# Output projections by Strassen's algorithm over pairs of token blocks, and stage buffers in pools that take turns

## The chip, the cores and the metric

The kernel runs on one core of a Trainium2 chip. Its engines are TensorE (PE; its weight loads are listed as PEld), VectorE (DVE), ScalarE (ACT) and GpSimd (POOL); SyncE (SP) issues nearly all transfers. Each engine works through its own queue in order and waits on semaphores. The metric is the device time of one execution in microseconds, as the median of several runs; a profiled execution gives the trace, whose span runs from the first to the last instruction.

## The reference

Two layers of gated attention over 2048 prompt tokens and 64 sample tokens, width 1024, 16 heads of 64. Layer 0 (here A) attends to a window of its own and two earlier chunks with two key/value heads and learned sinks; layer 1 (B) to its own and eight earlier chunks with 16 heads. In each layer the attention's output, times a gate, goes through a square output projection and is added to the layer's input:

```python
y_p = x_p + (op * jax.nn.silu(gp)) @ w_out      # (2048 x 1024) @ (1024 x 1024)
...
y_s = x_s + (os_ * jax.nn.silu(gs)) @ w_out     # (64 x 1024) @ (1024 x 1024)
```

Everything is float32. The outputs are the tokens after both layers and the newest keys and values.

## The kernel before, in words

All activations lie transposed (features on partitions, tokens along the free dimension). A product of two float32 matrices is made of three matmuls in a faster type: each operand is split into a high part (a cast on ScalarE) and a low part (the operand less its high part, on VectorE for weights, on GpSimd for activations), and high x high, high x low and low x high are added up in PSUM. So 128 rows of outputs, 128 features of input and one block of tokens cost three matmuls.

The order of TensorE's instructions is written out by hand. Attention is a pipeline over its items, and a `Filler` (L615) hands out matmuls of independent jobs between attention's steps, so that TensorE has work while VectorE and ScalarE do the softmax. Its jobs stand in one list: layer A's input projections, layer A's output projections, layer B's input projections, layer B's output projections. `Filler.to(mark)` runs jobs up to a mark; marks are sums of ideal matmul times. The other engines' queues are ordered by the framework's scheduler, which places an instruction by its own estimate of times.

The 2112 tokens are cut into 8 blocks of 264 (`OT`). An output job (`output_jobs`, L1251) is one block and one half of the 1024 output features: it loads the gated attention output of its block in four pieces of 256 features (`load_act`, L351; the piece `xraw` is cast at L385 and its low part made at L386), and for each of four groups of 128 output features runs 8 x 3 = 24 matmuls of 264 columns into one PSUM bank `pj` (L1283 to L1285), adds the layer's input `res` on VectorE (L1288) and stores pairs of groups (L1290). Weights of a half come in eight pieces of 512 columns, cast at L307, low part at L308. There are 16 such jobs in a layer, first the 8 blocks of half 0, then those of half 1. In each layer the last attention items are interleaved with the first output jobs, and the rest of the jobs runs alone. Layer B's input jobs need all of layer A's blocks that they read.

SBUF tiles of all stages come from one pool `sb`; keys, values and their low parts (`KA`, `KB`, `VT` and others) are constants that stay for the whole kernel. PSUM has the pools `pp` and, for attention, `pa` or `pb`.

## Time and profile before

| | |
|---|---|
| median of 3 runs | 2325.57 us (2324.6 to 2330.49) |
| profiled execution, span | 2323.8 us |
| matmuls | 13981, of which 3072 in output projections |
| TensorE busy | 2269.6 us |
| VectorE, ScalarE, GpSimd busy | 1547.3, 1432.7, 847.6 us |
| output projections from, to (layer A) | 659.4 to 863.2 us |
| output projections from, to (layer B) | 2110.7 to 2320.0 us |

The profiled execution's own time is its span; the median of the runs is 1.8 us above it. Matmuls are pipelined, so a matmul's duration is longer than the distance to the next one: what a matmul costs is read from the distance of starts. An engine's busy time includes time in which an instruction has started and cannot get on.

### The profile page before, as it was taken

The numbers are of one execution on the slowest core, as the hardware profiler recorded it, in microseconds if no ns is written. First come the engines' busy times: TensorE is split into PE (matmuls) and PEld (weight loads), VectorE is DVE, ScalarE is ACT, GpSimd is POOL, SyncE is SP. The second block draws the span as 40 slices with busy tenths as digits, with TensorE's granted clock in tenths as the row PEclk, the third lists the DMA queues.
The fourth block names the chain that finished last, engine by engine and source line by source line (L and its number), as shares of the span: only waits on it lengthen the run. The fifth ranks groups of instructions, "written<-read, shape, count | busy, mean of one in ns | idle before, by whom it ended". The sixth has DMA issues, their size and how long they took to land.

```text
span 2323.8 us, 42433 instructions
## 1 busy us (share of the span) xinstructions
PE 2269.6 (98%) x13981; PEld 1985.2 (85%) x13981; DVE 1547.3 (67%) x5214; ACT 1432.7 (62%) x3644; POOL 847.6 (36%) x1194
## 2 busy tenths in 40 slices
PE   8899999999999998999999999999999999999999
PEld 7787888888889997878888888888888888888999
DVE  7679988887782228876766767767667677676211
ACT  7778777777772236765665656656656566566321
POOL 5554533333254446432222222222222222224443
PEclk9999999999999999999999999999999999999999
DMA  8846446754446776453444533534435435433664
GB/s 256 263 146 207 162 144 195 229 167 162 134 126 204 226 216 219 145 186 126 158 142 128 161 127 114 178 126 152 143 123 163 134 103 177 131 126 106 189 186 148
DMA packets 232126, 379.37 MB, mean 163 GB/s; under 512 B 24721, under 2 KB 163361, under 8 KB 231873
## 3 DMA queue, kind: packets, MB, share of 16 engines
q1 hardware_dynamic: 231904, 376.65, 51.3%
q8 instruction: 110, 1.80, 0.3%
q14 instruction: 112, 0.91, 0.1%
HBM read 296.13 MB, written 82.08 MB: 163 GB/s over the span
## 4 chain that ended last, share of the span: by engine, by line
PE 77%; DVE 10%; ACT 5%; DMA 5%; issue 2%; POOL 1%; SPq 0%; POOLq 0%; ACTq 0%; DVEq 0%
PE pj L481 13%; PE pj L483 12%; PE pj L482 12%; PE pj L1283 5%; PE pj L1284 5%; PE pj L1285 5%; PE sb L597 5%; PE o L1189 3%; PE o L1188 3%; PE tp L597 3%; PE sb L1110 3%; PE sb L1111 3%; PE sa L597 2%; DVE sq L524 1%; DVE p L1114 1%
## 5 line engine op out<-in xcount | busy, mean ns | idle before, releaser
L481 PE MATMUL pj<-wh,xx 128*128 128x512 f32 (+1 forms) x1648 | 668.7, 406 | 15.2 <-DVE ms L433 7.2
L483 PE MATMUL pj<-wh,xx 128*128 128x512 f32 (+1 forms) x1648 | 638.1, 387 | 0.0
L482 PE MATMUL pj<-wl,xx 128*128 128x512 f32 (+1 forms) x1648 | 635.0, 385 | 0.0
L483 PEld LDWEIGHTS pj<-wh,xx 128*128 128x128 f32 x1648 | 310.4, 188 | 67.3
L481 PEld LDWEIGHTS pj<-wh,xx 128*128 128x128 f32 x1648 | 311.9, 189 | 56.9 <-ACT pb L504 6.5
L386 POOL TENSOR_TENSOR xx<-xraw,xx 128x528 fp32r<-128x528 f32 (+1 forms) x200 | 265.6, 1344 | 218.2 <-ACT xx L385 212.0
L482 PEld LDWEIGHTS pj<-wl,xx 128*128 128x128 f32 x1648 | 312.5, 190 | 37.7
L528 POOL TENSOR_TENSOR f<-f,mhalf 128x4 f32<-128x4 f32 (+3 forms) x221 | 227.9, 1031 | 228.7 <-DVE f L524 216.9
L1118 ACT ACTIVATE p<-p,nm 128x640 f32<-128x640 f32 (+5 forms) x272 | 204.4, 751 | 167.2 <-DVE nm L1114 165.1
L1283 PE MATMUL pj<-xx,wh 128*128 128x264 f32 x1024 | 293.3, 286 | 0.1
L1284 PE MATMUL pj<-xx,wh 128*128 128x264 f32 x1024 | 291.3, 284 | 0.0
L1285 PE MATMUL pj<-xx,wl 128*128 128x264 f32 x1024 | 289.8, 283 | 0.0
L1114 DVE CUSTOM_DVE_ANT_0 p<-sb,BT 128x640 f32<-128x640 f32 (+5 forms) x272 | 196.7, 723 | 119.6 <-PE sb L1111 116.2
L570 DVE TENSOR_TENSOR pl<-sb,ph 128x640 fp32r<-128x640 f32 (+5 forms) x288 | 196.8, 683 | 116.1 <-ACT ph L569 113.7
L385 ACT CAST xx<-xraw 128x528 fp32r<-128x528 f32 (+1 forms) x200 | 123.4, 626 | 220.3 <-PE pj L1285 131.9
L984 POOL TENSOR_TENSOR o<-gt,o 128x256 f32<-128x256 f32 (+2 forms) x140 | 107.4, 767 | 371.3 <-issue 149.0
L569 ACT CAST ph<-sb 128x640 fp32r<-128x640 f32 (+5 forms) x288 | 167.1, 580 | 122.4 <-PE sb L597 114.0
L1288 DVE TENSOR_TENSOR res<-pj,res 128x264 f32<-128x264 f32 x128 | 55.1, 431 | 246.5 <-PE pj L1285 230.7
L1283 PEld LDWEIGHTS pj<-xx,wh 128*128 128x128 f32 x1024 | 192.7, 188 | 0.8 <-DVE res L1288 0.3
L1285 PEld LDWEIGHTS pj<-xx,wl 128*128 128x128 f32 x1024 | 192.6, 188 | 0.0
L1284 PEld LDWEIGHTS pj<-xx,wh 128*128 128x128 f32 x1024 | 192.4, 188 | 0.2
L524 DVE CUSTOM_DVE_ANT_0 sq<-pa 128x64 f32<-128x64 f32 (+1 forms) x850 | 170.2, 253 | 22.1 <-ACT pa L504 20.0
(189 smaller groups left out, 4810.5 us busy)
## 6 DMA issues: line engine op xcount, KB each, us to landing
xx<-xsb SPq DMA_DIRECT2D x224, 512.0 KB, 4.1
xx<-xsa SPq DMA_DIRECT2D x88, 512.0 KB, 4.8
xraw<-oga SPq DMA_DIRECT2D x64, 264.0 KB, 3.4
xraw<-ogb SPq DMA_DIRECT2D x64, 264.0 KB, 3.3
xsa<-xx SPq DMA_DIRECT2D x32, 512.0 KB, 4.0
wraw<-in_w_in_b_dram SPq DMA_DIRECT2D x64, 256.0 KB, 3.4
xsb<-xx SPq DMA_DIRECT2D x32, 512.0 KB, 3.8
xraw<-in_x_dram SPq DMA_DIRECT2D x40, 256.0 KB, 4.1
```

The source lines that it names most:

```text
L386: nc.gpsimd.tensor_tensor(xl, rv, xh.bitcast(F32), op=ALU.subtract)
L481: nc.tensor.matmul(ps[:n, :C], xh, wh, start=k == 0, stop=False)
L482: nc.tensor.matmul(ps[:n, :C], xh, wl, start=False, stop=False)
L483: nc.tensor.matmul(ps[:n, :C], xl, wh, start=False, stop=k == KC - 1)
L528: nc.gpsimd.tensor_tensor(fv, fv, mhalf[:n, :H], op=ALU.pow)
L570: b = nc.vector.tensor_tensor(dst_lo, src, dst_hi.bitcast(F32), op=ALU.subtract)
L597: nc.tensor.transpose(out, in_, ident[:n, :n])
L1114: mi = nc.vector.tensor_tensor_reduce(out=p[:n, :nk], in0=S[:n, o : o + nk], in1=bias[:n, b0 : b0 + nk], op0=ALU.add, op1=ALU.min, scale=1 ...
L1118: ex = nc.scalar.activation(p[:n, :nk], p[:n, :nk], AF.Exp, scale=-1.0, bias=nmh, accum_out=it.sm[:n, 2 * i + h : 2 * i + h + 1],)
L1283: nc.tensor.matmul(ps[:, :OT], wh, oh, start=k == 0, stop=False)
L1284: nc.tensor.matmul(ps[:, :OT], wh, ol, start=False, stop=False)
L1285: nc.tensor.matmul(ps[:, :OT], wl, oh, start=False, stop=k == KC - 1)
```

## The change

Half 0 of the first four token blocks is still made directly (`FIRST = 4`). All other output blocks are made by Strassen's algorithm in the form with seven products and fifteen additions. A job is a pair of token blocks and one half of the output features: the operands are 2 x 2 blocks, (two token blocks) x (two halves of the input features) and (two halves of the input features) x (two groups of 256 output features). There are six such jobs in a layer, two in half 0 and four in half 1. A product is 24 matmuls of 264 columns into a PSUM tile `pw` of two banks.

- `weights(half, k)`: the operand of product k on the weights' side. Raw quarters `wq` are loaded once a half; sums and differences of them are made on VectorE, then each operand is split (cast on ScalarE, low part on VectorE).
- `operand(g)`: the same for activations. Raw quarters `oq` are loaded, sums `os` made on VectorE, and the split's low part goes to VectorE for the first of the operand's two pieces and to GpSimd for the second (`LOW_DVE`). Operands are made two products ahead (`AHEAD`).
- `add_job`: after the first product ScalarE copies it to `op1` and GpSimd adds it to three residual tiles `ores`; every later product, or sum of products in the same banks, is added to a residual tile by VectorE. Products 0 to 2 and so on share banks: with the letters "abababa", product 2 is accumulated on product 0's banks, 3 on 1's, 5 on 3's, 6 on 4's, so that a product waits until the addition of the one before it in its banks is done.
- `begin()` starts the stage: raw loads, all seven weight operands and two activation operands are issued while the rest of the direct jobs runs on TensorE.

Attention's tiles and those of the new stages come from pools that are opened and closed stage by stage (`PHASED`): attention A, output A, attention B, output B. A tile of a later stage waits for the tiles of the earlier one that lay in the same place. Constants of attention (`KA`, `VT`, ...) become tiles of their stage, and the queries' zero rows are written once a layer.

```diff
+FIRST = 4
+AHEAD = 2
+LOW_DVE = (0, 2, 4, 6, 8, 10, 12)
+PHASED = {
+    "p", "ph", "pl", "q1", "G", "gt", "o1", "pa", "pb", "sq", "f", "nm", "sm", "ko",
+    "oq", "os", "ores", "op1", "wq", "vh", "vl",
+}
...
-        return sb.tile(shape, dt, tag=tag, name=f"{tag}_{uid[0]}", bufs=bufs)
+        pool = phase[0] if tag in PHASED else sb
+        return pool.tile(shape, dt, tag=tag, name=f"{tag}_{uid[0]}", bufs=bufs)
...
 
-        for j in range(NO):
+        for j in range(FIRST):
             add_unit(j)
+
+    def wino_output(layer, xin, xout):
+        st = Item()
+        st.raw, st.res, st.A, st.q, st.w, st.parts = {}, {}, {}, {}, {}, {}
+        st.open = False
+        todo = [(0, p) for p in range(FIRST // 2, NO // 2)] + [(1, p) for p in range(NO // 2)]
+        w_o = (w_o_a, w_o_b)[layer]
+        T2 = 2 * OT
...
+        def split(src, hi, lo, dve):
+            nc.scalar.copy(hi, src)
+            e = nc.vector if dve else nc.gpsimd
+            e.tensor_tensor(lo, src, hi.bitcast(F32), op=ALU.subtract)
+
+        def weights_raw(half):
+            q = {}
+            for n, k in ((0, 0), (0, 1), (1, 0), (1, 1)):
+                q[n, k] = halves_of("wq", [P, 512], 12)
+                for c, r in enumerate(q[n, k]):
+                    src = w_o[half, 2 * k + c, :, :, 256 * n : 256 * n + 256]
+                    load(r.rearrange("p (k c) -> p k c", k=2), src)
+            st.q[half] = q
+
+        def weights(half, k):
+            q = st.q[half]
+            if k == 1:
+                q["d"] = halves_of("wq", [P, 512], 12)
+                q["s"] = halves_of("wq", [P, 512], 12)
+                for c in range(2):
+                    nc.vector.tensor_tensor(q["d"][c], q[1, 0][c], q[0, 0][c], op=ALU.subtract)
+                    nc.vector.tensor_tensor(q[1, 0][c], q[1, 1][c], q[1, 0][c], op=ALU.subtract)
+                    nc.vector.tensor_tensor(q["s"][c], q[1, 0][c], q[0, 0][c], op=ALU.add)
+            if k == 5:
+                for c in range(2):
+                    nc.vector.tensor_tensor(q["s"][c], q[0, 1][c], q["s"][c], op=ALU.subtract)
+            src = q[((0, 0), "s", (0, 1), (1, 0), "d", "s", (1, 1))[k]]
+            out = []
+            for c in range(2):
+                if k < 3:
+                    wh, wl = (t(n, [P, 2, 256], WN, F32R) for n in ("wh", "wl"))
+                else:
+                    wh, wl = (t(n, [P, 2, 256], 8, F32R) for n in ("vh", "vl"))
+                split(src[c], wh.rearrange("p k c -> p (k c)"), wl.rearrange("p k c -> p (k c)"), True)
+                out.append((wh, wl))
+            st.w[half, k] = out
...
+        def operand(g):
+            i, k = divmod(g, 7)
+            if i >= len(todo):
+                return
+            A = lambda tb, kb: st.A[i, tb, kb]
+            for c in range(2):
+                if k == 1:
+                    if c == 0:
+                        st.A[i, "s1"] = halves_of("os", [P, T2], 4)
+                        st.A[i, "s2"] = halves_of("os", [P, T2], 4)
+                    s1, s2 = st.A[i, "s1"][c], st.A[i, "s2"][c]
+                    nc.vector.tensor_tensor(s1, A(1, 0)[c], A(1, 1)[c], op=ALU.add)
+                    nc.vector.tensor_tensor(s2, s1, A(0, 0)[c], op=ALU.subtract)
+                elif k == 3:
+                    a = A(1, 0)[c]
+                    nc.vector.tensor_tensor(a, A(0, 0)[c], a, op=ALU.subtract)
+                elif k == 6:
+                    s2 = st.A[i, "s2"][c]
+                    nc.vector.tensor_tensor(s2, A(0, 1)[c], s2, op=ALU.subtract)
+            key = ((i, 0, 0), (i, "s2"), (i, 0, 1), (i, 1, 0), (i, "s1"), (i, 1, 1), (i, "s2"))[k]
+            out = []
+            for c, a in enumerate(st.A[key]):
+                xx = t("xx", [P, 4 * OT], XN, F32R)
+                split(a, xx[:, :T2], xx[:, T2:], 2 * k + c in LOW_DVE)
+                out.append((pair(xx[:, :T2]), pair(xx[:, T2:])))
+            st.parts[g] = out
+
+        def begin():
+            st.open = True
+            half = todo[0][0]
+            weights_raw(half)
+            raw(0, (0, 0), (1, 0), (1, 1), (0, 1))
+            residual(0)
+            for k in range(7):
+                weights(half, k)
+                if k < AHEAD:
+                    operand(k)
+                filler.to(min(filler.direct, filler.done + 2.2))
+            filler.to(filler.direct)
+
+        def add_job(i):
+            half, p = todo[i]
+            last = i + 1 < len(todo) and todo[i + 1][0] != half
+
+            def gen():
+                bank = {}
+                view = lambda x: x.rearrange("p (n c) -> p n c", n=2)[:, :, :OT]
+
+                def add(x, r):
+                    nc.vector.tensor_tensor(pair(r), view(bank[x]), pair(r), op=ALU.add)
+
+                def done(tb, nb):
+                    c, o = 4 * half + 2 * nb, (2 * p + tb) * OT
+                    store(xout[:, c : c + 2, o : o + OT], pair(st.res[i, tb, nb]))
+
+                for k in range(7):
+                    g = 7 * i + k
+                    x = "abababa"[k]
+                    if k in (0, 1, 4):
+                        bank[x] = psum("pw", 1024, 2, scores_pool[0])
+                    if k == 2:
+                        raw(i + 1, (0, 0), (1, 0))
+                    elif k == 3:
+                        raw(i + 1, (1, 1))
+                        residual(i + 1)
+                    elif k == 4:
+                        raw(i + 1, (0, 1))
+                    if last and k == 0:
+                        weights_raw(1)
+                    if last and k > 0:
+                        weights(1, k - 1)
+                    if i and k == 0 and todo[i - 1][0] != half:
+                        weights(1, 6)
+                    operand(g + AHEAD)
+                    parts = st.parts.pop(g)
+                    w = st.w[half, k]
+                    first, final = k in (0, 1, 4), k in (2, 5, 6)
+                    for n in range(2):
+                        dst = bank[x][:, 512 * n : 512 * n + OT]
+                        for c in range(4):
+                            oh, ol = (a[:, c % 2, :] for a in parts[c // 2])
+                            wh, wl = (a[:, c % 2, n * P : (n + 1) * P] for a in w[c // 2])
+                            nc.tensor.matmul(dst, wh, oh, start=first and c == 0, stop=False, skip_group_check=True)
+                            nc.tensor.matmul(dst, wh, ol, start=False, stop=False, skip_group_check=True)
+                            nc.tensor.matmul(dst, wl, oh, start=False, stop=c == 3, skip_group_check=True)
+                            if n < 1 or c < 3:
+                                yield 3 * OT / 2400
+                    r = lambda tb, nb: st.res[i, tb, nb]
+                    if k == 0:
+                        p1 = t("op1", [P, T2], 2)
+                        nc.scalar.copy(pair(p1), view(bank[x]))
+                        for tb, nb in ((0, 1), (1, 1), (1, 0)):
+                            nc.gpsimd.tensor_tensor(r(tb, nb), r(tb, nb), p1, op=ALU.add)
+                    elif k == 1:
+                        add(x, r(0, 1))
+                    elif k == 2:
+                        add(x, r(0, 0))
+                        done(0, 0)
+                    elif k == 3:
+                        add(x, r(1, 1))
+                    elif k == 4:
+                        add(x, r(1, 1))
+                        done(1, 1)
+                    elif k == 5:
+                        add(x, r(1, 0))
+                        done(1, 0)
+                    else:
+                        add(x, r(0, 1))
+                        done(0, 1)
+                        for j in (2 * p, 2 * p + 1):
+                            key = ("x1", "y")[layer], j
+                            finished[key] = finished.get(key, 0) + 1
+                    yield 3 * OT / 2400
...
     with tc.manual_schedule(engines={mybir.EngineType.PE}):
         attend_a = layer_a()
-        for half in range(2):
-            output_jobs(0, half, x0, x1)
+        output_jobs(0, 0, x0, x1)
+        direct_a = filler.total
+        output_a = wino_output(0, x0, x1)
         attend_b = layer_b()
-        for half in range(2):
-            output_jobs(1, half, x1, y)
-        with tc.tile_pool(name="pa", bufs=4, space=bass.MemoryType.PSUM) as scores_pool[0]:
-            attend_a()
-        with tc.tile_pool(name="pb", bufs=2, space=bass.MemoryType.PSUM) as scores_pool[0]:
-            attend_b()
-        filler.attending = False
-        filler.to(filler.total)
+        output_jobs(1, 0, x1, y)
+        direct_b = filler.total
+        output_b = wino_output(1, x1, y)
+        for name, work, direct in (
+            ("a", attend_a, None), ("wa", output_a, direct_a), ("b", attend_b, None), ("wb", output_b, direct_b)
+        ):
+            filler.direct = direct
+            filler.attending = False
+            with tc.tile_pool(name="s" + name, bufs=1, reuse_waits="tile") as phase[0]:
+                bufs = 4 if name == "a" else 2
+                with tc.tile_pool(name="p" + name, bufs=bufs, space=bass.MemoryType.PSUM, reuse_waits="tile") as scores_pool[0]:
+                    work()
```

On the engines, the rows show what stands one behind another in a queue. A row is the line, the operation, what it writes and reads, and the size of a row of the output. VectorE before, in the middle of layer A's output jobs (`res` residuals, `pj` a job's PSUM bank, `wl` the low part of weights):

```order
L1288 TENSOR_TENSOR res_10223<-pj_10277,res_10223 128x264
L1288 TENSOR_TENSOR res_10304<-pj_10306,res_10304 128x264
L308 TENSOR_TENSOR wl_10256<-wraw_9987,wh_10255 128x512
L308 TENSOR_TENSOR wl_10263<-wraw_9997,wh_10262 128x512
L308 TENSOR_TENSOR wl_10270<-wraw_10007,wh_10269 128x512
L1288 TENSOR_TENSOR res_10304<-pj_10332,res_10304 128x264
```

Between the weights there are only additions out of PSUM. VectorE now, where layer A's new stage begins (L1307 is the direct jobs' addition, the old L1288; L1338 a low part; L1355 to L1357 sums of weights; L1405 sums of operands; `wl`, `vl` low parts of weights, `xx` of operands):

```order
L1307 TENSOR_TENSOR res_9760<-pj_9762,res_9760 128x264
L1355 TENSOR_TENSOR wq_9697<-wq_9628,wq_9620 128x512
L1356 TENSOR_TENSOR wq_9628<-wq_9632,wq_9628 128x512
L1307 TENSOR_TENSOR res_9760<-pj_9796,res_9760 128x264
L1357 TENSOR_TENSOR wq_9699<-wq_9628,wq_9620 128x512
L1355 TENSOR_TENSOR wq_9698<-wq_9629,wq_9621 128x512
L1338 TENSOR_TENSOR vl_9785<-wq_9628,vh_9784 128x512
L1338 TENSOR_TENSOR xx_9668<-oq_9636,xx_9668 128x528
L1356 TENSOR_TENSOR wq_9629<-wq_9633,wq_9629 128x512
L1338 TENSOR_TENSOR wl_9708<-wq_9699,wh_9707 128x512
L1357 TENSOR_TENSOR wq_9700<-wq_9629,wq_9621 128x512
L1405 TENSOR_TENSOR os_9715<-oq_9640,oq_9644 128x528
```

Sums and low parts of weights stand around the last direct additions; the low part of the first operand, `xx`, comes after eight of the weights' rows. VectorE now, in the middle of the new stage of layer B (L1443 is the addition of a product out of PSUM; L1405 to L1412 are sums of operands):

```order
L1405 TENSOR_TENSOR os_29175<-oq_29025,oq_29061 128x528
L1443 TENSOR_TENSOR ores_28803<-pw_28987,ores_28803 128x528
L1409 TENSOR_TENSOR oq_29025<-oq_29021,oq_29025 128x528
L1338 TENSOR_TENSOR xx_29073<-oq_28797,xx_29073 128x528
L1443 TENSOR_TENSOR ores_28801<-pw_28951,ores_28801 128x528
L1338 TENSOR_TENSOR xx_29111<-os_28913,xx_29111 128x528
L1406 TENSOR_TENSOR os_29177<-os_29175,oq_29021 128x528
L1405 TENSOR_TENSOR os_29176<-oq_29026,oq_29062 128x528
L1409 TENSOR_TENSOR oq_29026<-oq_29022,oq_29026 128x528
L1443 TENSOR_TENSOR ores_28807<-pw_28987,ores_28807 128x528
L1338 TENSOR_TENSOR xx_29143<-oq_29021,xx_29143 128x528
L1406 TENSOR_TENSOR os_29178<-os_29176,oq_29022 128x528
```

The additions out of PSUM now stand between sums and low parts of the next products' operands, those of the next job among them. GpSimd now, where the new stage of layer A begins (L397 is the direct jobs' low part, the old L386; L1338 the low part of the second piece of an operand; L1486 the addition of the first product, `op`, to a residual tile):

```order
L397 TENSOR_TENSOR xx_9500<-xraw_9492,xx_9500 128x528
L1338 TENSOR_TENSOR xx_9671<-oq_9637,xx_9671 128x528
L1486 TENSOR_TENSOR ores_9654<-ores_9654,op_2144_9935 128x528
L1486 TENSOR_TENSOR ores_9656<-ores_9656,op_2144_9935 128x528
L1486 TENSOR_TENSOR ores_9658<-ores_9658,op_2144_9935 128x528
L1338 TENSOR_TENSOR xx_9726<-os_9718,xx_9726 128x528
L1338 TENSOR_TENSOR xx_9908<-oq_9649,xx_9908 128x528
L1338 TENSOR_TENSOR xx_9946<-oq_9641,xx_9946 128x528
```

The three additions of the first product stand ahead of the second product's low part (`xx<-os`).

More of the change, by code (lines that the diff above doesn't have):

```diff
@@ L599, in hybrid_encoder_kernel @@
     halves = [slice(0, 64), slice(64, 128)]
-    Q2 = [const([P, 512], f"q2_{i}", F32R) for i in range(2)]
     turn = [0]
@@ L605, in zero @@
         nc.gpsimd.memset(x.bitcast(F32), 0.0)
-    for q in Q2:
-        zero(q[64:128])
     def low_queries():
         turn[0] += 1
-        return Q2[turn[0] % 2]
+        return own.Q2[turn[0] % 2]
     class Filler:
@@ L700, in take_kv @@
                 kn, v = pr[:n, 0:128], pr[:n, 128:256]
-                split_v(n, v, VS[:, 1] if last else VT[:, tt])
+                split_v(n, v, own.VS[:, 1] if last else own.VT[:, tt])
                 it.knorm = head_norm(n, kn)
@@ L941, in pipeline @@
         def pipeline():
+            attention_tiles("a")
+            for q in own.Q2:
+                zero(q[64:128])
             N = len(items)
@@ L1023, in gen @@
                     v, kn = pr[:n, 256:384], pr[:n, 128:256]
-                    split_v(n, v, VS[:, 2] if last else VT[:, tt])
+                    split_v(n, v, own.VS[:, 2] if last else own.VT[:, tt])
                     it.todo += head_norm(n, pr[:n, 0:256]) + gate(n, it.gate[:n, e])
@@ L1055, in queries @@
             if u == NU:
[L1056 removed]
+                kd = [a[:, CB : CB + TS] for a in (own.KSA, own.KSB)]
             else:
[L1058 removed]
+                kd = [a[:, u * UT : (u + 1) * UT] for a in (own.KA, own.KB)]
             qt = [tp[r, 0:T] for r in halves]
@@ L1201, in pipeline @@
             bg.lazy = True
-            for q in Q2:
+            attention_tiles("b")
+            for q in own.Q2:
+                zero(q[64:128, 0:256])
                 zero(q[0:64, 256:512])
```

99 lines of the change are left out of this document (70 added, 29 removed).

## The prediction

> **What bounds the kernel now.** I read the page's busy times and its chain first, then the two output stages in stretches of time, then each kind of instruction that the change multiplies, and last the stretches in which VectorE and GpSimd work at once.
>
> ```profile
> PE 2269.6 (98%) x13981; PEld 1985.2 (85%) x13981; DVE 1547.3 (67%) x5214; ACT 1432.7 (62%) x3644; POOL 847.6 (36%) x1194
> ...
> PE 77%; DVE 10%; ACT 5%; DMA 5%; issue 2%; POOL 1%; SPq 0%; POOLq 0%; ACTq 0%; DVEq 0%
> ```
>
> TensorE is busy 98% and holds 77% of the chain, so a matmul less is time less, as long as nothing else takes over. The change touches only the output projections. Two stretches inside them (columns: length, then busy us and count by engine, granted clock, DMA share, GB/s):
>
> ```profile
> 720.00:840.00 120.00, 120.00 (x989) 120.00 (x988) 24.42 (x49) 31.78 (x51) 54.07 (x41) 1.00 0.68 203
> 2210.00:2310.00 100.00, 100.00 (x825) 100.00 (x824) 17.38 (x37) 22.30 (x36) 43.71 (x33) 1.00 0.62 178
> ```
>
> TensorE never waits there: 120/989 = 0.121 us a matmul of 264 columns. VectorE is 20% busy, GpSimd 45%. What VectorE does there waits for TensorE, hardly the reverse:
>
> ```profile
> L1288 DVE TENSOR_TENSOR res<-pj,res x128: 400/433/436, 669.6 to 2320.3; 128x264 f32<-128x264 f32 x128
> ...
>   PE pj L1285: 230.7, 100
> ...
>   PEld pj L1283: 0.3, 1
> ```
>
> Where the stages begin and end: the last attention matmul of a layer, and the last output matmul (durations min/median/max, then first and last start, first for layer A, then for layer B).
>
> ```profile
> L931 PE MATMUL o<-pl,VT x22: 389/397/505, 607.5 to 705.6; 128*128 128x512 f32 x22
> L1285 PE MATMUL pj<-xx,wl x512: 278/282/292, 659.7 to 863.2; 128*128 128x264 f32 x171
> ```
>
> ```profile
> L1189 PE MATMUL o<-pl,VT x36: 273/280/334, 2106.2 to 2166.1; 128*128 128x256 f32 x24, 128*128 128x128 f32 x12
> L1285 PE MATMUL pj<-xx,wl x512: 278/282/290, 2111.0 to 2320.0; 128*128 128x264 f32 x171
> ```
>
> So the stretch after attention is 863.2 - 705.6 = 157.6 us in layer A and 2320.0 - 2166.1 = 153.9 us in layer B. The instructions stand in the same order as before on every compute engine outside these stretches, so I leave the rest of the span as it is.
>
> **What is removed.** A layer's projections take 2 x 8 x 96 = 1536 matmuls; now 4 x 96 direct and 6 x 168 in products, 1392. That is 144 x 0.121 = 17.4 us a layer, 34.8 us in all, if TensorE stays the bound.
>
> **What is added, per layer.** VectorE gets 28 low parts of weights, 16 sums of weights, 42 low parts of operands and 48 sums of operands: 134 instructions that read two SBUF tiles, where before there were 8 (the second half's weights, L308). It gets 36 additions out of PSUM of 528 columns for 48 of 264. GpSimd has 42 low parts and 18 additions of the first product, 60 for 48. ScalarE has 15 casts or copies of 528 in a job of seven products. Prices:
>
> ```profile
> L308 DVE TENSOR_TENSOR wl<-wraw,wh x32: 674/693/1825, 512.9 to 2226.5; 128x512 fp32r<-128x512 f32 x32
> L386 POOL TENSOR_TENSOR xx<-xraw,xx x200: 1262/1327/1816, 5.1 to 2307.2; 128x528 fp32r<-128x528 f32 x64, 128x512 fp32r<-128x512 f32 x36
> L385 ACT CAST xx<-xraw x200: 602/633/642, 4.4 to 2306.5; 128x528 fp32r<-128x528 f32 x64, 128x512 fp32r<-128x512 f32 x36
> L570 DVE TENSOR_TENSOR pl<-sa,ph x132: 403/680/693, 60.4 to 702.4; 128x512 fp32r<-128x512 f32 x124, 128x256 fp32r<-128x256 f32 x4, 64x256 fp32r<-64x256 f32 x4
> ```
>
> ScalarE: 15 x 0.63 = 9.5 us in a job whose matmuls take 168 x 0.121 = 20.3 us; never the bound. Transfers: activations and residuals as many as before (64 and 32 a layer), weights 24 for 16; at a landing of 3.4 us they were hidden and stay so once the stage runs.
>
> ```profile
> xraw<-oga SPq DMA_DIRECT2D x64, 264.0 KB, 3.4
> ```
>
> VectorE's first line has a strange spread: median 0.69 us, longest 1.83. The timeline of both engines shows why (start, duration).
>
> ```profile
> 757.11 3.91 POOL L386 TENSOR_TENSOR xx<-xraw,xx 128x528 fp32r<-128x528 f32 x3 [5.14 <-ACT xx L385]
> ```
>
> ```profile
> 769.28 4.40 POOL L386 TENSOR_TENSOR xx<-xraw,xx 128x528 fp32r<-128x528 f32 x3 [5.64 <-ACT xx L385]
> ```
>
> ```profile
> 768.18 1.29 DVE L308 TENSOR_TENSOR wl<-wraw,wh 128x512 fp32r<-128x512 f32 x2 [0.46 <-ACT wh L307]
> 769.76 1.45 DVE L308 TENSOR_TENSOR wl<-wraw,wh 128x512 fp32r<-128x512 f32 x1 [0.28 <-ACT wh L307]
> 771.13 0.42 DVE L1288 TENSOR_TENSOR res<-pj,res 128x264 f32<-128x264 f32 x1
> ```
>
> Three GpSimd instructions alone take 3.91 us, 1.30 each. At 769.76 a VectorE instruction with two SBUF tiles starts behind the first of the three: it takes 1.45 instead of 0.69, and the three take 4.40. They do not overlap; each stands until the other is done. At 771.13 VectorE's addition out of PSUM runs under GpSimd's third instruction at its usual 0.42. So a **pair**, one such VectorE and one GpSimd instruction with both queues full, costs 1.30 + (4.40 - 3.91) = 1.79 us of VectorE's queue. Alone, VectorE's instruction costs 0.61 (two in 1.29, the second ending 0.6 after the first), the addition out of PSUM of 528 columns about 0.62 (0.68 for 512, less the same overlap).
>
> [...]
>
> **The sum.** Per layer VectorE has 60 pairs, 107.4 us; the other 70, once the first four are done, 42.7 us; 36 additions out of PSUM, 22.3 us: 172.4 us in one queue. It cannot start at once: its fifth weight instruction stands behind a direct addition that waits for TensorE, 93 matmuls after attention in layer A (11.3 us), 66 in layer B (8.0 us). In layer A 16 instructions for layer B's first unit and its weights and 4 GpSimd low parts fall in as well: 16 x 0.61 + 4 x 1.18 = 14.5 us. So the stretch lasts 11.3 + 172.4 + 14.5 = 198.2 us in layer A, 8.0 + 172.4 = 180.4 us in layer B. TensorE alone would need 17 + 122 = 139 us. Against 157.6 and 153.9 that is **+40.6 and +26.5, together +67.1 us**: the 34.8 us are lost, and as much twice over. On the profiled execution, 2323.8 + 67.1 = 2390.9; its median run is 2325.57, 1.8 above its span, hence **2392.7, say 2393 us**.
>
> Bounds. Above: all pairs collide as summed and TensorE's own waits add to it. At each start GpSimd's three additions of the first product stand ahead of the low part that the second product needs: product one ends, copy 0.6, three times 1.30, then 1.30: product two starts about 5 us late even with no collision. Where TensorE idles long its clock falls:
>
> ```profile
> 1003.00:1010.00 7.00, 3.47 (x20) 2.75 (x18) 6.62 (x20) 2.09 (x5) 1.77 (x4) 0.90 0.93 316
> 1010.00:1017.00 7.00, 7.00 (x30) 6.33 (x31) 2.86 (x13) 4.03 (x9) 3.22 (x5) 0.61 0.23 73
> ```
>
> After 3.5 us idle the granted clock is 0.61 over the next 7 us, some 2.7 us lost. Five such waits a layer would be 27 us; I take none, because VectorE and not TensorE sets the pace while these waits occur, and keep 20 us for the range. Below: no pair collides. Then VectorE needs 130 x 0.61 + 22.3 = 102 us, TensorE decides, and only the late second product (5 us) and the job in which the second half's weights are made (37 x 0.61 + 6 x 0.62 = 26.3 us for 20.3) are lost: 17.4 - 11 = 6.4 us gained a layer, 13 in all. I take the upper end, because both queues are long and in order, and nothing makes GpSimd wait for VectorE's gaps.
>
> The pools that take turns: the first weights land where old keys lay, the first operands where the last values lay, so those loads wait for attention's last matmul. 17 us of direct matmuls cover them (3.4 us each landing, 16 in a row): zero, up to 5 us a layer where the queue is slow. At the end a single 528 column addition stands for one of 264, +0.2 us.
>
> **Rivals.**
> - *Half hidden.* GpSimd's instructions run under the 36 PSUM additions and while VectorE waits for casts. For it: at 771.13 they do overlap. Against: GpSimd too waits for casts, and the adds stand between others. It takes at most 22.3 us a layer off: 2393 - 45 = 2348 us.
> - *TensorE stays the bound* (the other side). Collisions are rare since the engines drift apart. Decisive count in layer A: 11.3 + 102 + 14.5 + 1.18 c = 157.6 gives c = 25 of 60; under some 25 to 40 collisions a layer is no longer than before. At none: 2325.6 - 13 = 2313 us; with the start's waits hidden too, 2291. For it: GpSimd is idle a third of a job (10 x 1.30 = 13 us of 20.3). Against: VectorE is then at 15 x 0.61 + 6 x 0.62 = 12.9 us of the same 20.3, the two sums with the pairs' loss do not fit in 20.3, and the weights' job is over it already.
> - *The waits add up.* Loads at the start and the falling clock come on top: 2393 + 20 = 2413, at worst 2430 us.
>
> **How the numbers follow.** Forecast (2370 to 2412) 0.58, half hidden 0.20, the waits add up 0.12, TensorE stays the bound 0.10. About 0.3%, 7 us, is what a measurement of this kernel tells from no change. Faster takes 0.07 of the last case; within 0.3% takes its remaining 0.03 and 0.02 of the half hidden one; slower has 0.88. The range, 2345 to 2425, leaves out the last case and the tops of the third.
>
> **What would show it.** Right: in the two stretches VectorE is busy nearly throughout, its low parts and sums of 512 and 528 average about 1.2 us ((60 x 1.79 + 70 x 0.61)/130, plus the overlap) for 0.69 alone, GpSimd's about 1.7; TensorE idles some 59 and 45 us there, waiting for DVE, most of it at the start and in the job with the weights; attention's stretches keep their length. Wrong: VectorE's instructions at 0.7 us, or TensorE without waits in the products, or waits on DMA of the raw operands in place of DVE.

## The result, and the profile after

The changed kernel takes **2399.58 us** (median of 4 runs, 2397.91 to 2399.86), the kernel before 2325.62 us (2324.6 to 2330.49): 1.0312 times as long, 95% interval 1.0298 to 1.0327, or 74 us more. The prediction said 2393 us, 2345 to 2425, slower with 0.88. The total is close, but by luck: two errors in the sum behind it cancel, as shown below.

The busy times on the changed kernel's page:

```profile
PE 2266.9 (95%) x13693; PEld 1976.0 (82%) x13693; DVE 1802.3 (75%) x5442; ACT 1502.7 (63%) x3768; POOL 920.9 (38%) x1220
```

TensorE has 288 matmuls fewer, worth 288 x 0.121 = 34.8 us, and only 2.7 us less busy time: many of its matmuls now run at a lower clock (granted 0.91 and 0.90 over the two stages, 1.00 in the prediction's windows of the kernel before). VectorE has 228 instructions more and 255 us more. Where the stages begin and end, by the same two kinds of matmul as before (last attention matmul, last output matmul; layer A, then layer B):

```profile
L945 PE MATMUL o<-pl,VT_a x2: 397/399/401, 704.7 to 705.1; 128*128 128x512 f32 x2
L1478 PE MATMUL pw<-xx,vl x192: 278/284/422, 748.6 to 907.5; 128*128 128x264 f32 x192
...
L1206 PE MATMUL o<-pl,VT_b x36: 272/278/333, 2145.6 to 2205.6; 128*128 128x256 f32 x24, 128*128 128x128 f32 x12
L1478 PE MATMUL pw<-xx,vl x192: 278/283/422, 2250.7 to 2393.1; 128*128 128x264 f32 x192
```

Layer A's stretch is 907.5 - 705.1 = 202.4 us (157.6 before), layer B's 2393.1 - 2205.6 = 187.5 us (153.9 before): +44.8 and +33.6, and some 5 us less between them. TensorE's waits in the products (total, times, longest):

```profile
  PE pw L1476 <- DVE ores L1443: 46.8, 22, 5.9
  PE pw L1477 <- DVE xx L1338: 14.0, 4, 7.1
  PE pw L1477 <- POOL xx L1338: 12.4, 8, 5.3
  PE pw L1476 <- ACT xx L1336: 7.3, 3, 3.4
```

That is 80.5 us, most of it for VectorE's addition of an earlier product. Both engines in layer B's fourth job show why that addition is late: first VectorE, then GpSimd (start, duration).

```profile
2333.93 1.82 DVE L1406 TENSOR_TENSOR os<-os,oq 128x528 f32<-128x528 f32 x1
2335.68 1.84 DVE L1405 TENSOR_TENSOR os<-oq,oq 128x528 f32<-128x528 f32 x1
2337.55 1.68 DVE L1409 TENSOR_TENSOR oq<-oq,oq 128x528 f32<-128x528 f32 x1
2339.16 0.69 DVE L1443 TENSOR_TENSOR ores<-pw,ores 128x528 f32<-128x528 f32 x1
2339.78 0.69 DVE L1338 TENSOR_TENSOR xx<-oq,xx 128x528 fp32r<-128x528 f32 x1
```

```profile
2331.63 1.81 POOL L1338 TENSOR_TENSOR xx<-os,xx 128x528 fp32r<-128x528 f32 x1
2333.40 1.78 POOL L1338 TENSOR_TENSOR xx<-oq,xx 128x528 fp32r<-128x528 f32 x1
2335.14 1.81 POOL L1338 TENSOR_TENSOR xx<-os,xx 128x528 fp32r<-128x528 f32 x1
2336.91 1.76 POOL L1338 TENSOR_TENSOR xx<-oq,xx 128x528 fp32r<-128x528 f32 x1
```

The two engines take turns: GpSimd starts every 1.74 to 1.77 us, VectorE's sums last 1.68 to 1.84 us, and once GpSimd is done a VectorE instruction with two SBUF inputs lasts 0.69. The prediction's price of a pair (one instruction of each engine) was 1.79; the rows show about 1.75. The additions like the one at 2339.16 read PSUM and are not slowed (all 72 last 693 to 709 ns, beside GpSimd or not), but this one stands behind three sums of the next job. TensorE waited for it, and paid twice (its first matmul after the wait, with the wait in brackets; then windows: length, busy us and count of PE, PEld, DVE, ACT, POOL, granted clock, DMA share, GB/s):

```profile
2340.00 0.56 PE L1476 MATMUL pw<-xx,vh 128*128 128x264 f32 x1 [3.39 <-DVE ores L1443]
```

```profile
2339.70:2343.10 3.40, 3.10 (x15) 3.13 (x16) 3.33 (x6) 0.00 (x0) 0.00 (x0) 0.53 0.42 115
2343.10:2346.50 3.40, 3.40 (x31) 3.40 (x30) 2.00 (x3) 1.27 (x2) 1.34 (x1) 1.00 0.70 205
```

After 3.4 us without a matmul TensorE is busy 3.10 us with 15 matmuls, at a granted clock of 0.53, where 15 x 0.121 = 1.8 us would do: 3.4 us idle, and some 1.3 us more at about half clock. In the window after that the clock is 1.00 again.

### The profile page after: what moved, and what is told of

The parts are those of the page before. It is cut to its first block, busy times and chain, and to the rows that moved or that the text cites. A ratio compares the mean times of both kernels' runs of the same rounds, so it can differ in the third digit from the quotient of the medians.

```text
span 2397.2 us, 42397 instructions
## 1 busy us (share of the span) xinstructions
PE 2266.9 (95%) x13693; PEld 1976.0 (82%) x13693; DVE 1802.3 (75%) x5442; ACT 1502.7 (63%) x3768; POOL 920.9 (38%) x1220
## 3 DMA queue, kind: packets, MB, share of 16 engines
q8 instruction: 108, 1.77, 0.3%
## 4 chain that ended last, share of the span: by engine, by line
PE 48%; DVE 8%; issue 2%; ACT 2%; DMA 1%; POOL 1%; SPq 0%; POOLq 0%; DVEq 0%; ACTq 0%
PE pj L492 9%; PE pj L494 8%; PE pj L493 8%; PE sb L615 5%; PE o L1206 3%; PE o L1205 3%; PE sb L1127 2%; PE sb L1128 2%; PE tp L615 2%; DVE p L1131 1%; PE pw L1476 1%; PE pw L1477 1%; PE pw L1478 1%; DVE xx L1338 1%; DVE pl L588 1%
## 5 line engine op out<-in xcount | busy, mean ns | idle before, releaser
L1001 POOL TENSOR_TENSOR o<-gt,o 128x256 f32<-128x256 f32 (+2 forms) x140 | 106.7, 762 | 368.8 <-issue 157.7
L615 PEld LDWEIGHTS sb<-ident,p 128*128 128x128 f32 (+2 forms) x1168 | 139.5, 140 | 52.6 <-issue 12.4
L908 ACT ACTIVATE p<-p,nm 128x257 f32<-128x257 f32 (+2 forms) x272 | 134.5, 497 | 74.3 <-DVE nm L902 62.8
L615 PE MATMUL sb<-ident,p 128*128 128x128 f32 (+2 forms) x1168 | 171.6, 272 | 7.9 <-DVE nm L1131 5.4
L515 ACT ACTIVATE pa<-pj,rms 128x384 f32<-128x384 f32 (+1 forms) x206 | 111.1, 539 | 93.1 <-PE pj L494 90.5
L1205 PE MATMUL o<-ph,VT_b 128*128 128x256 f32 (+1 forms) x672 | 167.5, 285 | 0.0
L397 POOL TENSOR_TENSOR xx<-xraw,xx 128x512 fp32r<-128x512 f32 (+1 forms) x104 | 138.1, 1338 | 59.2 <-ACT xx L396 55.4
L1206 PE MATMUL o<-pl,VT_b 128*128 128x256 f32 (+1 forms) x672 | 156.6, 281 | 2.6 <-DVE pl L588 2.6
L1000 DVE TENSOR_TENSOR o<-o,o 64x256 f32<-64x256 f32 (+2 forms) x280 | 112.1, 400 | 56.2 <-ACT o L998 49.0
L1476 PE MATMUL pw<-xx,vh 128*128 128x264 f32 x384 | 115.1, 300 | 36.0 <-DVE ores L1443 36.0
```

The costliest lines, as they stand in the source:

```text
L615: nc.tensor.transpose(out, in_, ident[:n, :n])
L1205: nc.tensor.matmul(dst, vt, it.ph[h][:kn, c, q0:q1_], start=x == 0, stop=False)
L1206: nc.tensor.matmul(dst, vt, it.pl[h][:kn, c, q0:q1_], start=False, stop=x == len(mm) - 1)
```

## The experiments

Theory: a VectorE instruction with two SBUF inputs and a GpSimd instruction exclude each other, as in the turns of 1.74 to 1.77 us above; that fills VectorE's queue and makes TensorE wait. Rivals: VectorE simply has too many instructions; GpSimd's own results come late; the scheduler put the queues in a bad order; the start of a stage (loads, pools) or the falling clock. Each stretch below is taken as above, from the run's profiled execution; a line's number shifts by a few from kernel to kernel. From `all_vector` on, the ratios are to runs of the kernel before beside them on the same chip, 2326.9 to 2328.9 us.

| kernel | layer A us | layer B us | time us | ratio, 95% interval |
|---|---|---|---|---|
| before | 157.6 | 153.9 | 2325.62 | 1 |
| changed | 202.4 | 187.5 | 2399.58 | 1.0312 (1.0298 to 1.0327) |
| all_vector | 178.2 | 164.8 | 2352.93 | 1.0109 (1.0094 to 1.0124) |
| lows_gpsimd | 213.1 | 195.5 | 2422.29 | 1.042 (1.0391 to 1.0449) |
| gpsimd_empty | 159.1 | 150.7 | 2322.75 | 0.9978 (0.9967 to 0.999) |
| sums_out | 161.1 | 145.1 | 2317.6 | 0.9953 (0.9938 to 0.9968) |
| after_order | 203.3 | 193.6 | 2406.6 | 1.034 (1.0326 to 1.0354) |
| vector_order | 185.9 | 169.2 | 2365.51 | 1.0162 (1.0148 to 1.0176) |
| pools_alone | 167.2 | 153.8 | 2333.6 | 1.0026 (1.0015 to 1.0036) |
| half1_vector | 177.4 | 161.6 | 2347.96 | 1.0085 (1.007 to 1.01) |
| half1_early | 179.6 | 161.4 | 2350.56 | 1.0086 (1.0069 to 1.0103) |
| half1_gpsimd | 195.0 | 176.3 | 2379.39 | 1.0217 (1.0201 to 1.0233) |
| half1_order | 167.1 | 149.3 | 2329.73 | 1.0014 (1.0005 to 1.0023) |
| b_half1 | 157.3 | 150.2 | 2322.45 | 0.9975 (0.9966 to 0.9984) |

### Work moved between VectorE and GpSimd

The first, `all_vector`, gives VectorE 60 instructions a layer more and takes all of the products' work from GpSimd:

```diff
-LOW_DVE = (0, 2, 4, 6, 8, 10, 12)
+LOW_DVE = range(14)
...
-    nc.gpsimd.tensor_tensor(r(tb, nb), r(tb, nb), p1, op=ALU.add)
+    nc.vector.tensor_tensor(r(tb, nb), r(tb, nb), p1, op=ALU.add)
```

> All of GpSimd's work in the products goes to VectorE: the 42 low parts of operands and the 18 additions of the first product a layer. Theory (a VectorE instruction with two SBUF inputs and a GpSimd instruction exclude each other, and that is what makes VectorE too slow): VectorE gets 60 instructions a layer more and is still faster, 194 x 0.61 + 36 x 0.62 = 141 us a layer for 172, now about TensorE's own 139; about 35 us a layer less than the changed kernel: 2325 us (2310 to 2345), VectorE's low parts and sums at about 0.69 us on average. Rival (VectorE simply has too many instructions in one ordered queue, exclusion or not): 60 more at about 0.7 us, +42 us a layer where VectorE sets the pace throughout, +20 where only in the first half of a stage: 2440 to 2485 us.

The second, `lows_gpsimd`, goes the other way: `LOW_DVE = ()`.

> The opposite move: all 84 low parts of operands a layer on GpSimd, VectorE has 42 instructions a layer fewer. Theory (exclusion): 92 instructions of VectorE with two SBUF inputs meet 102 of GpSimd; up to 92 pairs x 1.79 + 36 x 0.62 = 187 us a layer for 172, and GpSimd alone needs 17 x 1.30 = 22 us in a job of 20.3: 2400 to 2440 us, slower than the changed kernel or equal though VectorE has less to do. Rival (too many instructions on VectorE): 42 x 0.7 = 29 us a layer less: 2340 to 2365 us.

More work for VectorE made the stages shorter, 2353 us, and less work made them longer, 2422 us. Both rule out the rival that VectorE just has too many instructions (2440 or more, and 2340 to 2365). The two stretches of the changed kernel, of `all_vector` and of `lows_gpsimd` (same columns as above):

```profile
705.00:908.00 203.00, 157.69 (x1154) 153.21 (x1153) 167.63 (x194) 84.69 (x143) 106.84 (x68) 0.91 0.59 185
2206.00:2394.00 188.00, 152.18 (x1122) 148.67 (x1120) 157.50 (x177) 71.04 (x120) 104.52 (x62) 0.90 0.54 166
```

```profile
705.00:883.00 178.00, 149.81 (x1150) 145.60 (x1149) 156.47 (x254) 83.75 (x143) 10.04 (x8) 0.94 0.66 211
2180.00:2346.00 166.00, 145.84 (x1127) 143.00 (x1125) 145.97 (x237) 71.05 (x120) 1.75 (x2) 0.94 0.60 189
```

```profile
706.00:920.00 214.00, 160.02 (x1155) 154.48 (x1154) 149.22 (x152) 82.81 (x143) 171.04 (x110) 0.88 0.56 177
2217.00:2413.00 196.00, 156.78 (x1125) 150.95 (x1124) 137.15 (x135) 69.63 (x120) 164.21 (x104) 0.90 0.51 160
```

With 254 instructions VectorE is busy 156 us in layer A, with 194 beside GpSimd 168. But `all_vector` was forecast at 2325 us and missed by 28, outside its range. VectorE is busy 156 of 178 us in layer A and no longer throughout, yet TensorE still waits in the products, 28 us in layer A and 20 in B, mostly in the first job for operands' low parts and casts, then for additions. In `lows_gpsimd` the forecast (187 us of VectorE's queue besides the starts, 2400 to 2440 us) was met, 213 and 195.5 us a stretch, though not in the way that it was worked out: VectorE is busy 149 of 214 us and GpSimd 171, so it is GpSimd that is nearest to full there.

### GpSimd's work left out, VectorE's sums left out

`gpsimd_empty` leaves GpSimd's instructions out and gives them to nobody:

```diff
-            e = nc.vector if dve else nc.gpsimd
-            e.tensor_tensor(lo, src, hi.bitcast(F32), op=ALU.subtract)
+            if dve:
+                nc.vector.tensor_tensor(lo, src, hi.bitcast(F32), op=ALU.subtract)
...
-                out.append((pair(xx[:, :T2]), pair(xx[:, T2:])))
+                out.append((pair(xx[:, :T2]), pair(xx[:, T2:] if low else xx[:, :T2])))
...
-                        for tb, nb in ((0, 1), (1, 1), (1, 0)):
-                            nc.gpsimd.tensor_tensor(r(tb, nb), r(tb, nb), p1, op=ALU.add)
```

> Leaves out GpSimd's 42 low parts of operands (the high part is used in their place) and its 18 additions of the first product a layer; VectorE's, ScalarE's and TensorE's work stays as in the changed kernel. Theory (exclusion): VectorE needs 134 x 0.61 + 36 x 0.62 = 104 us a layer, TensorE's 139 decide, with 5 to 12 us a layer lost at the start: 2305 us (2295 to 2330). Rival (the start's loads, the late casts and the falling clock make the loss; or VectorE's backlog of weights alone): nothing of that changes, 2360 us or more.

`sums_out` keeps GpSimd as it is and takes the sums from VectorE:

```diff
-                    s1, s2 = st.A[i, "s1"][c], st.A[i, "s2"][c]
-                    nc.vector.tensor_tensor(s1, A(1, 0)[c], A(1, 1)[c], op=ALU.add)
...
+            if k == 1:
+                st.A[i, "s1"], st.A[i, "s2"] = A(1, 0), A(0, 0)
```

> Leaves out the fifteen-additions' operand part: VectorE's 16 sums of weights and 48 sums of operands a layer (unsummed blocks are used in their place); GpSimd's 60 instructions, the low parts, the 36 additions out of PSUM and TensorE's matmuls stay. Theory (exclusion fills VectorE's queue): a job is now 7 pairs x 1.79 + 6 x 0.62 = 16.3 us of VectorE for TensorE's 20.3, so TensorE decides outside the start: 2325 us (2312 to 2345), though GpSimd does exactly what it did. Rival (GpSimd's own low parts and additions come late, whatever VectorE does): GpSimd is as long as before, 2375 us or more.

Both leave out work that the result needs, so they serve to measure and not to use. Either one suffices: 2322.75 and 2317.6 us, inside their ranges, though `gpsimd_empty` was expected at 2305; the rivals' 2360 and 2375 us or more fall. In `gpsimd_empty` VectorE executes the same instructions as in the changed kernel:

```profile
706.00:866.00 160.00, 146.52 (x1155) 143.88 (x1154) 120.44 (x194) 83.42 (x143) 9.28 (x8) 0.97 0.74 235
2163.00:2315.00 152.00, 143.14 (x1124) 141.63 (x1123) 112.11 (x177) 71.07 (x120) 1.51 (x2) 0.96 0.65 206
```

Its 194 and 177 instructions take 120.4 and 112.1 us in place of 167.6 and 157.5: GpSimd's presence costs VectorE 47.2 and 45.4 us, and the stretches 43.3 and 36.8 us. In `sums_out` GpSimd's work is nearly as long as in the changed kernel, and harmless:

```profile
708.00:870.00 162.00, 145.93 (x1155) 142.80 (x1154) 116.68 (x130) 83.62 (x143) 102.58 (x68) 0.99 0.73 233
2167.00:2314.00 147.00, 140.41 (x1130) 139.18 (x1128) 95.66 (x113) 71.09 (x121) 94.94 (x62) 0.98 0.67 214
```

So GpSimd's own lateness is not the cause. One kind of instruction, VectorE's low part of an operand that is a raw block (in `sums_out` all are), in layer B's stretch, in the changed kernel, in `gpsimd_empty` and in `sums_out` (count, busy us, mean ns):

```profile
L1338 DVE TENSOR_TENSOR xx<-oq,xx 128x528 fp32r<-128x528 f32 x24 | 26.7, 1113 | 0.0
```

```profile
L1338 DVE TENSOR_TENSOR xx<-oq,xx 128x528 fp32r<-128x528 f32 x24 | 16.8, 702 | 0.0
```

```profile
L1338 DVE TENSOR_TENSOR xx<-oq,xx 128x528 fp32r<-128x528 f32 x42 | 47.7, 1139 | 8.9 <-ACT xx L1336 8.6
```

In `sums_out` the collisions go on, 1139 ns a piece; with fewer instructions VectorE has room for them. It is the collisions together with the number of instructions that make the loss: taking away either one removes it.

### The order of the queues

`after_order` holds the products' VectorE instructions behind the last addition that the program wrote before them, and their loads behind the last direct residual's load:

```diff
-  nc.vector.tensor_tensor(s1, A(1, 0)[c], A(1, 1)[c], op=ALU.add)
+  behind(nc.vector.tensor_tensor(s1, A(1, 0)[c], A(1, 1)[c], op=ALU.add).ins, held["add"])
...
-  nc.vector.tensor_tensor(pair(r), view(bank[x]), pair(r), op=ALU.add)
+  held["add"] = nc.vector.tensor_tensor(pair(r), view(bank[x]), pair(r), op=ALU.add).ins
```

> The changed kernel with the same instructions, but sums, low parts and the loads of the products are held in VectorE's and SyncE's queues behind the last addition or residual load that the program wrote before them (the scheduler had drawn up to four sums of the next pair ahead of an addition that TensorE waits for). Theory (exclusion makes VectorE's queue too long, whatever its order): the first three jobs of a stage stay as they are, at most the one stall of 3.4 us in each of the later jobs goes: 2380 to 2400 us. Rival (the order of VectorE's queue makes the loss): the 46.8 us of waits for the additions go, and the half clock with them: 2345 us or less.

`vector_order` puts the same ordering on `all_vector`:

> The same ordering for the kernel that has all of GpSimd's work in the products on VectorE (2353 us). Theory (what is left there is VectorE's capacity at the start: 44 instructions for weights and the first job's 25 + 6, 46 us, in the 37 us of direct matmuls and the first job; and 22 more in the job before the second half): 10 to 20 us a layer stay lost, 2338 us (2328 to 2352). Rival (order alone): 2325.6 - 34.8 - 4.8 + 10 = 2296, at most 2315 us.

Both got slower, 2406.6 us for 2399.6 and 2365.5 for 2352.9, and both lie above the theory's ranges. TensorE's waits of `after_order` in layer A:

```profile
PE pw L1480 <- DVE xx L1339: 20.9, 5, 8.3
PE pw L1480 <- POOL xx L1339: 15.8, 12, 5.1
...
PE pw L1479 <- DVE ores L1446: 1.0, 2, 0.7
```

The waits for the additions are nearly gone, 1.0 us (5.9 in layer B), and come back as waits for the operands that were now prepared later. The line of a wait names what happened to be last, not the cause. The rival, that the scheduler's order makes the loss, falls by far (2345 us or less, and 2315 or less); that no third order would do better is not shown. The theory takes a blow too: in `after_order` VectorE is busy 11 and 14 us less than in the changed kernel (156 and 144 us), and the stretches are no shorter. So the length of VectorE's work alone doesn't set them; when each operand is ready counts as well. How much of what remains in `vector_order` is VectorE's capacity at the start stays unproved.

### The pools alone, and other divisions

`pools_alone` keeps the pools of the change and returns to direct products everywhere:

```diff
-        for j in range(FIRST):
+        for j in range(NO):
             add_unit(j)
...
-        output_a = wino_output(0, x0, x1)
+        output_jobs(0, 1, x0, x1)
+        end_a = filler.total
+        output_a = lambda: filler.to(end_a)
```

> Only the pools that take turns, with the direct products of the kernel before for all of both halves. Theory: no gain or loss in the output stages, and the 4.8 us that the trace of the changed kernel shows between the two stages stay: 2321 us (2318 to 2328). Rival (part of the loss is the pools': buffers come free late at each phase): 2335 us or more.

It took 6 us more, with an interval that excludes no change: above the forecast's range, below the rival's 2335 us. Layer B's stretch is what it was; layer A's is 9.6 us longer, and the time between the two stretches 4.7 us shorter (1298.2 us for 1302.9). At the end of layer A, SyncE (transfers it issues):

```profile
856.17 0.46 SPq L400 DMA_DIRECT2D xsb<-xx  x1
...
860.22 0.43 SPq L382 DMA_DIRECT2D xraw<-x  x1
860.68 1.73 SPq L1297 DMA_DIRECT2D res<-in_x_dram  x2
```

The last residual's loads stand behind layer B's first transfers, and TensorE's longest wait in that stretch is for the addition to them (total, times, longest):

```profile
PE pj L1302 <- DVE res L1307: 7.7, 2, 7.2
```

So the pools alone cost something only where a phase closes, and the rows point to the order of SyncE's queue; in the changed kernel TensorE has no wait of this kind.

Next, seven products for the second half of the output columns alone, behind 8 direct jobs for the first half. `half1_vector` is `all_vector` with `FIRST = 8` and the weights' preparation from 18 us ahead; `half1_early` begins it 38 us ahead; `half1_gpsimd` is `half1_early` with the changed kernel's division of the work:

```diff
-FIRST = 4
+FIRST = 8
...
+            filler.to(filler.direct - 38.0)
             for k in range(7):
                 weights(half, k)
-                if k < AHEAD:
-                    operand(k)
-                filler.to(min(filler.direct, filler.done + 2.2))
+                filler.to(min(filler.direct, filler.done + 3.5))
+            for k in range(AHEAD):
+                operand(k)
+                filler.to(min(filler.direct, filler.done + 2.2))
```

> Seven products for the second half of the output columns alone (96 matmuls a layer saved for 144), all of GpSimd's work in them on VectorE, weights and first operands prepared under the last 18 us of direct matmuls. Theory (without exclusion only the start is lost, since VectorE's 44 instructions for weights and its first low parts do not fit under that cover): 2325.6 - 2 x 11.6 - 4.8 (layer B's attention, as in the changed kernel) + 2 x 18 (the first job's loss in the run with everything on VectorE) = 2333 us (2320 to 2340). Rival (the loss is a per-job one): 2298 + 8 jobs x 4.5 = 2334 us; the two differ in where TensorE waits, and in the next run.

> As the run before, but the weights are prepared from 38 us ahead of the first product, in 3.5 us steps, the operands behind them. Theory: the start's loss is gone, 2325.6 - 23.2 - 4.8 = 2298 us (2293 to 2312), faster than the kernel before. Rival (the loads of a new phase, or a per-job loss): no change against the run before, 2325 us or more.

> As the run before, but with the changed kernel's division: seven of fourteen low parts and the three additions of the first product a job on GpSimd. Theory (exclusion): a job costs VectorE 10 x 1.79 + 5 x 0.61 + 6 x 0.62 = 24.7 us for TensorE's 20.3, 8 jobs x 4.4 = 35 us more than the run before: 2333 us (2322 to 2345). Rival (exclusion hurts only where weights and operands pile up at a start): within 8 us of the run before.

GpSimd's share again costs 29 us (2379.4 for 2350.6, 15 a layer, 3.6 a job where 4.4 was expected), far from the rival's 8. But my reading of the start fell, and with it all three forecast times: 2333 and 2298 us were expected of the first two, 2348 and 2351 came, and beginning earlier changed nothing. TensorE stands still once in each layer, for 17.4 and 16.7 us, at the direct addition's line. The wait of layer A in `half1_early`, and SyncE at that time:

```profile
PE pj L1302 <- DVE res L1307: 17.4, 1, 17.4
```

```profile
710.49 5.24 SPq L1346 DMA_DIRECT2D wq<-in_w_o_a_dram  x8
715.77 5.24 SPq L1381 DMA_DIRECT2D oq<-oga  x8
721.37 4.02 SPq L1391 DMA_DIRECT2D ores<-in_x_dram  x4
...
729.50 2.55 SPq L1381 DMA_DIRECT2D oq<-oga  x4
...
735.38 1.11 SPq L1297 DMA_DIRECT2D res<-in_x_dram  x2
```

The new pool's buffers are all free at once, so the scheduler issues every load that fits them, the next job's included, and a direct job's residual comes 25 us later. `half1_order` does three things: it spreads the weights over 46 us, loads the first operands and residuals later, and holds these loads and VectorE's sums and low parts behind the direct jobs' last residual load and addition:

> Seven products for the second half alone, all on VectorE, weights spread from 46 us ahead of the products, loads and VectorE's instructions held behind those of the direct matmuls that the program wrote before them. Theory (the 17 us waits of the two runs before were the direct residual's load behind 32 loads of the new phase, and its addition behind the weights' instructions): both waits go, 2350 - 2 x (17 + 3.4 at half clock) = 2309 us, 2298 where nothing else is lost (2296 to 2315), faster than the kernel before. Rival (the new phase's loads are late whatever their order): a wait of 10 us or more stays at each start, 2325 us or more.

The long waits go (2.2 us at most remain for those additions in a layer), and the time falls by 21 us to 2329.7, 3 us above the kernel before. The forecast, 2296 to 2315 us, is missed. Its sum takes 3.4 us at half clock for each long wait; that is the author's estimate, and the one wait taken apart above, of 3.39 us, cost some 1.3. Which of the three things did how much of the 21 us was not tried apart. Layer B's stretch is now shorter than before (149.3 for 153.9), layer A's still longer (167.1 for 157.6). `b_half1` therefore uses it in layer B alone and lets layer A's direct products run in layer B's phase:

```diff
-  output_a = wino_output(0, x0, x1)
+  output_jobs(0, 1, x0, x1)
...
-  ("a", attend_a, None), ("wa", output_a, direct_a), ("b", attend_b, None)
+  ("a", attend_a, None), ("b", attend_b, None)
```

> Layer A's projections as in the kernel before and in one phase with layer B's attention; seven products for layer B's second half alone, as in the run before (all on VectorE, weights spread, order held). Theory: layer A's stretch is 157.6 us again (167.1 in the run before, where layer B's preparation shares VectorE and ScalarE with the products), layer B's stays 149.3 for 153.9: 2325.6 - 4.6 = 2321 us, 2316 where the 4 to 5 us in layer B's attention come too (2313 to 2325). Rival (a phase switch costs some us wherever it is, and the gain in layer B is only moved): 2326 to 2332 us, no faster than the kernel before.

```profile
L1304 PE MATMUL pj<-xx,wl x512: 278/282/292, 660.1 to 863.3; 128*128 128x264 f32 x171
L945 PE MATMUL o<-pl,VT_a x14: 389/397/499, 643.1 to 706.0; 128*128 128x512 f32 x14
...
L1485 PE MATMUL pw<-xx,vl x128: 279/283/422, 2241.3 to 2315.4; 128*128 128x264 f32 x128
L1206 PE MATMUL o<-pl,VT_b x12: 275/278/281, 2154.7 to 2165.2; 128*128 128x256 f32 x8, 128*128 128x128 f32 x4
```

Layer A's stretch is 157.3 us and layer B's 150.2. At 2322.45 us, 0.9975 of the kernel before, it is faster than both kernels, by little, and inside its forecast: 6 us where the 96 matmuls left out in layer B are worth 11.6.

## Why the prediction was right, point by point

**Direction, and the exclusion as its cause: shown.** Without GpSimd's instructions, or without the sums, the loss of 74 us is gone; more work on VectorE and none on GpSimd takes 47 us of it away.

**Price of a pair: right.** 1.79 us was summed; where the two engines take turns, a turn lasts 1.74 to 1.77.

**Number of pairs: too high.** I let all 60 of a layer collide. VectorE's extra time against `gpsimd_empty`, 47.2 and 45.4 us, at 1.79 - 0.61 = 1.18 each, is 40 and 38 pairs, an estimate. The reason given, that both queues are long and nothing makes GpSimd wait for VectorE's gaps, failed: GpSimd is busy 106.8 us of the 203, and its low parts wait 44 us of the rest for ScalarE's casts. VectorE's busy time was put at 172.4 + 14.5 = 186.9 us in layer A and 172.4 in layer B; it is 167.6 and 157.5.

**VectorE busy nearly throughout: wrong in the later jobs.** I gave it 11.3 and 8.0 us of idle time, all at the start; it has 35 and 30. The start is about right, 10.7 us idle up to 747 and 9.6 up to 2249. Then VectorE is full, and in the later jobs it is not: there the other 25 and 21 us lie (layer B: the end of the first job with the second, the third, the fourth):

```profile
2249.00:2295.00 46.00, 35.95 (x262) 34.82 (x261) 45.88 (x53) 19.35 (x33) 22.76 (x14) 0.93 0.48 143
2295.00:2325.00 30.00, 26.70 (x205) 26.13 (x204) 28.55 (x32) 12.23 (x21) 17.63 (x11) 0.94 0.58 173
2325.00:2350.00 25.00, 21.61 (x167) 21.43 (x166) 21.32 (x21) 9.08 (x15) 16.27 (x10) 0.93 0.64 178
```

The step that failed is "I take none [of the clock's loss], because VectorE and not TensorE sets the pace". The engines wait for each other in turn: VectorE's additions wait for products that TensorE runs at a low clock (0.53 in the window above) after it has waited for VectorE. VectorE's longest waits in the two stretches (total, times, longest):

```profile
DVE ores L1443 <- PE pw L1478: 17.2, 10, 3.5
```

```profile
DVE ores L1443 <- PE pw L1478: 12.8, 10, 2.3
```

The granted clock is 0.91 and 0.90 over the stretches. Their 1154 and 1122 matmuls would take 139.6 and 135.8 us at 0.121 and are busy 157.7 and 152.2: some 18 and 16 us go to the low clock, 34 together where the prediction took none and kept 20 for the range. With the 40 and 38 pairs its own sum would be 11.3 + 102 + 14.5 + 47.2 = 175 us in layer A and 8.0 + 102 + 45.4 = 155 in layer B; the 27 and 32 us up to the measured stretches are what it had left out. This is the mechanism of the rival "the waits add up", inside the forecast's total.

**The sum.** Layer A: 186.9 + 11.3 = 198.2 was predicted, 167.6 + 35 = 202.4 came (within rounding of the windows). Layer B: 172.4 + 8.0 = 180.4, against 157.5 + 30 = 187.5. Some 15 to 19 us too many for VectorE's work and 22 to 24 too few for its waits; with the 5 us gained between the stages, 2393 for 2399.6. That the total was met does not confirm its parts. One small sum of the prediction is off as well and changes nothing: the late second product is 0.6 + 3.9 + 1.3 = 5.8 us and not 5.

**What would show it.** Low parts and sums were to average 1.2 us; the low parts of layer B's operands in the row above average 1.11, all 134 by the same view 1.04 (1.02 in layer A). GpSimd's 1.7: its low parts 1.63 and 1.59 in layers A and B, its additions 1.70 and 2.10. TensorE's waits, 59 and 45 us: 80.5 together, the rest of its loss at the low clock. Attention's stretches were to keep their length: the time between the stages is 4.8 us shorter. `pools_alone` has 4.7 of it without any product, so it comes with the pools; how isn't known.

**The lower bound was too kind.** With no pair colliding I expected some 13 us of gain; `gpsimd_empty` shows 5, and `all_vector`, which collides with nothing either but has 60 instructions a layer more on VectorE, loses 25. What was missing lies mainly in the first jobs of a stage, which need more of VectorE than TensorE's time allows: in `gpsimd_empty` VectorE is busy all 60 us from 725 to 785, and TensorE waits there. How that loss divides between VectorE, the casts and the loads isn't settled.

**The pools.** "Zero, up to 5 us a layer": 6 us in all in `pools_alone`, 9.6 more at the end of layer A and 4.7 less between the stages; the wait is for a residual that was issued late, and not for the new stage's first loads.

## What to carry to other kernels

A matmul saved by additions is paid on another engine; price those additions with what else runs then, here up to 1.85 us and 1.03 on average, and not 0.7, for a VectorE instruction with two SBUF inputs beside GpSimd. Price, too, what a wait costs the engine that was meant to gain: here 34 us at a low clock. Where two engines take turns, as these do at 1.74 to 1.77 us, giving all the work to the faster one (0.69 us alone for 1.30) can be quicker than sharing it, as `all_vector` shows with 2353 us for 2400. Opening a pool of buffers at a stage's start lets the scheduler issue all loads that fit (in `half1_early` a residual's load came 25 us later for it); hold them behind those that the running stage still needs.

## What was not expected of the hardware

GpSimd is not always given its turn. At layer B's start VectorE runs a dozen instructions with two SBUF tiles one after the other at 0.69 us or less each, while three additions of GpSimd (3.9 us alone) stand for 11.4 us, the longest for 8.0 (rows of VectorE's run, then GpSimd's three additions, then all of its additions: min/median/max):

```profile
2230.05 0.69 DVE L1406 TENSOR_TENSOR os<-os,oq 128x528 f32<-128x528 f32 x1
...
2234.95 0.69 DVE L1409 TENSOR_TENSOR oq<-oq,oq 128x528 f32<-128x528 f32 x1
```

```profile
2228.84 11.42 POOL L1486 TENSOR_TENSOR ores<-ores,op 128x528 f32<-128x528 f32 x3 [4.10 <-ACT op L1484]
```

```profile
L1486 POOL TENSOR_TENSOR ores<-ores,op x36: 1317/1778/7998, 727.7 to 2380.3; 128x528 f32<-128x528 f32 x36
```

A hundred microseconds later the two take strict turns, 1.74 to 1.77 us each in the rows from 2331 us on. What decides between the two ways stays open; it may be one reason why fewer pairs cost VectorE time than were summed.
